# Differences of w_down quarters for the Strassen down projection: made on GpSimd in up passes 1 and 2 and kept in DRAM, instead of made during the down projection

## The chip, the cores and the metric

One Trainium2 chip, and of it one core. The metric is the device time of one execution in microseconds (us), as the median of several executions. A time in a row of the trace is counted from the start of the profiled span.

## The reference, cut to what matters

The whole is one inference step of a small trunk (one layer, 128 prompt tokens and 2048 latent tokens, width 1024): modulation, an input projection, attention and a state-space scan, an output projection, and then a feed-forward network with a centred convolution of width 3. The change touches the last product of that network only:

```python
def conv_ffn(h, w_up, conv_w, conv_b, w_down):
    ...
    g, val = jnp.split(acc + conv_b, 2, axis=-1)
    return (jax.nn.silu(g) * val) @ w_down

xs = xs + gt2[:, None, :] * conv_ffn(h, w_up[l], conv_w[l], conv_b[l], w_down[l])
y_sample = rms_norm(xs, g_final)
```

w_down has D_FF = 2816 rows and 1024 columns; everything is fp32.

## The kernel before, in words

**How fp32 is multiplied.** An operand is split into two fp32r parts: ScalarE (ACT) copies it into an fp32r tile, VectorE (DVE) subtracts that copy from the original and keeps the rest. Each product then is three matmuls (high x high, high x low, low x high). "A split" below means this pair of one ACT and one DVE instruction on 128 x 512 numbers.

**Up** (`ffn_up`, L1237). h @ w_up is a Strassen-Winograd product with 7 products in the place of 8. It goes over 66 units (c, fb): three passes c over the tokens, in each 22 blocks fb of the 2816 columns. A unit is 7 products (numbers 0 to 6; product 0 of the next unit is issued ahead, between this unit's 4 and 5). In pass 0 the sums of the weights are made and split, and the split tiles are written to DRAM (`wsd`, L1233); passes 1 and 2 only split three blocks per unit (one of them with its subtraction on GpSimd, POOL, L1231) and load the other four tiles from `wsd` (`w<-wsd`, L1228, 512 KB each). The gated result `th` is made on POOL (L1262) twice per unit and stored to `ffd` in DRAM (L1263). In passes 0 and 1, in the blocks 4, 8, 12 and 16, `combos` (L1142) loads 732 KB of tokens of the next pass, makes four differences of 128 x 366 numbers on POOL, and stores 732 KB.

**Down** (`ffn_down`, L1535). ff @ w_down is a Strassen-Winograd product, too. The 22 row blocks of w_down are taken as 11 pairs (block k of the upper half, block k of the lower half); a pair and the two column halves of 512 give four quarters of 128 x 512: two of the upper half (columns left and right) and two of the lower half. Three passes p take 3, 4 and 4 pairs (`KS`, `K0`, L64). Within a pass the 16 latent token blocks are taken two at a time as units u = 0 to 7, and u = 8 is the prompt. A step (p, u, g) is product g (0 to 6) of a unit: 9 matmuls per step in pass 0 and 12 in passes 1 and 2 (`down_product`, L1522). Units 0 and 1 (with 8 in pass 0) are interleaved step by step, and so are 6 and 7 in passes 0 and 1; the order is `down_steps`, L1389.

Product g needs its weights `dW[g, k]` (split tiles) for each pair k. Products 0, 1 and 5 use a quarter as it is; 2, 3, 4 and 6 use differences of quarters. These are made in the down stage: `down_fetch` (L1427) loads quarters into three raw places, `down_split` (L1433, instructions on L1438 ACT and L1439 DVE) splits one, and `down_sum` (L1441, instruction on L1444) subtracts in place, on POOL, or on DVE for two of the four in passes 1 and 2. `down_builds` (L1446) writes the order out: splits, sums and a few late fetches, each waiting for the one before it in the same raw place. They are issued two or three per step by `some` (L1634, called on L1685), for pass p + 1 as soon as the last unit pair of pass p has used a weight tile (`through`). For pass 0 the quarters are fetched at the end of up (L1308, L1313, L1314).

The token side: `down_prep` (L1493) makes the operand of a step as a split (`da`, `stg`: L1483 ACT, L1484 DVE) and changes the raw tokens between operands with two POOL instructions at g = 0 (L1503, L1504) and two at g = 3 (L1506, L1507); `down_tasks` (L1487) gives each its lead in steps. The results go from the PSUM banks X, Y, Z through ACT (`snap`, L1588) and DVE (`put`, L1621 to L1627) into tiles x; in passes 0 and 1 POOL starts an accumulating DMA of x into `x1d` (L1624), and x is free when that has landed. There are three such tiles in pass 0 (L1547).

**What sets the order.** PE, ACT, DVE and POOL run their instructions in the order of the program (L1940); each queue waits at its head. The SP queue, which starts nearly all DMAs, is ordered by the compiler's own schedule, and it waits at its head as well.

Of the kernel before, what the change touches and what calls it, by code (L numbers as in the profile page):

```python
# [9 lines left out]
F32 = mybir.dt.float32  # L10
# [7 lines left out]
D = 1024  # L18
# [57 lines left out]
class Kernel:  # L76
# [1160 lines left out]
    def ffn_up(self, first, p, pp, xp):  # L1237
# [46 lines left out]

        for u, (c, fb) in enumerate(units):
# [6 lines left out]
            if fb in (4, 8, 12, 16) and c < 2:  # L1292
                if fb == 4:
                    todo = self.combos(c + 1)
                next(todo)
            z = pp.tile([128, 512], F32, name="Z", bufs=3)
# [101 lines left out]
    def down_room(self):  # L1398
# [9 lines left out]
        self.dR = [None, None, self.upr.tile([128, 4, 512], F32, name="S", bufs=1)]  # L1408
# [4 lines left out]
        self.dW = {(n // 3, n % 3): pair[:, 1024 * n:1024 * n + 1024].rearrange("p (a c) -> p a c", a=2) for n in range(5)}  # L1413

    def down_raws(self):

        for n in (0, 1):
            t = [self.upr.tile([128, 8, 128], F32, name="upraw", bufs=4).rearrange("p a b -> p (a b)") for _ in range(2)]
            self.dR[n] = t

    def down_quarter(self, p, n, k):
        if n == 3:
            n, k = (0, (k + 3) % 4) if p else ((0, 3), (1, 3), (0, 0))[k]
        t = self.dR[n]
        return t[:, k] if n == 2 else t[k // 2][:, 512 * (k % 2):512 * (k % 2) + 512]

    def down_fetch(self, p, n, row, col, ks=None):  # L1427

        for k in range(KS[p]) if ks is None else ks:
            r0 = (11 * row + K0[p] + k) * 128  # L1430
# [572 lines left out]
```

## Time and profile before

| what | us |
|---|---|
| median of 3 runs | 2597.81 |
| lowest and highest of the 3 | 2597.65, 2606.19 |
| the profiled execution's own time | 2601.17 |
| its span, first to last instruction | 2599.4 |
| up passes 1 and 2 in the span, about | 1475 to 2109 |
| down in the span, about | 2109 to 2599 |

The rows further down come from the profiled execution. A row of a timeline has the start in us, the time taken, the engine, the source line, the operation, the tiles (written <- read), shape and number; in brackets stands how long the engine was idle before it and which instruction released it. A row of stretches has, for each engine, busy us and in brackets the number of instructions.

### The profile page before, as it was taken

How to read it: one execution, taken by the hardware profiler on the slowest of the kernel's cores; microseconds unless marked ns; L12 is line 12 of the kernel's file. 1: busy time of each engine (PE TensorE's matmuls, PEld its weight loads, DVE VectorE, ACT ScalarE, POOL GpSimd, SP SyncE). 2: the span in 40 equal slices, each digit the busy share in tenths (PEclk: the TensorE clock that was granted, in tenths of full speed). 3: DMA queues.
4: the chain of work that ended last, by engine and by line, in shares of the span. 5: the costliest groups of instructions: out<-in, count | busy, mean ns of one | idle time of the engine just before them, and what ended most of it. 6: DMA issues, size and time to landing. Idle time of an engine off the chain costs nothing.

```text
span 2599.4 us, 38577 instructions
## 1 busy us (share of the span) xinstructions
PE 2370.9 (91%) x12997; PEld 2091.8 (80%) x12997; DVE 1949.3 (75%) x3283; ACT 1409.3 (54%) x2894; POOL 1290.9 (50%) x1565
## 2 busy tenths in 40 slices
PE   6976997799999878879999999999999999899998
PEld 3765786588888557669999899998999978688787
DVE  6899766887777796778888866666666676966986
ACT  6643556877777575665555644445444453433443
POOL 2687403667767754756666533234222255635343
PEclk8988998899999999989999999999999999999999
DMA  7554754411111547977777877778667658575653
GB/s 243 175 165 147 208 158 132 161 60 68 68 66 46 118 135 257 262 215 253 266 257 252 301 258 264 243 278 293 225 228 245 220 167 178 114 189 100 176 186 110
DMA packets 281368, 486.63 MB, mean 187 GB/s; under 512 B 43737, under 2 KB 166737, under 8 KB 281041
## 3 DMA queue, kind: packets, MB, share of 16 engines
q1 hardware_dynamic: 266481, 457.41, 54.1%
q0 software_dynamic: 9792, 17.83, 4.6%
q10 hardware_dynamic: 4896, 8.92, 1.0%
q8 instruction: 103, 1.69, 0.3%
q14 instruction: 96, 0.79, 0.1%
HBM read 318.84 MB, written 162.86 MB: 185 GB/s over the span
## 4 chain that ended last, share of the span: by engine, by line
PE 47%; DVE 15%; ACT 7%; issue 7%; DMA 4%; POOL 4%; SPq 0%; ACTq 0%; POOLq 0%; DVEq 0%
PE X L1197 13%; PE X L1528 7%; PE Z L1197 6%; PE Z L1528 4%; PE Y L1197 4%; PE pt L1009 3%; DVE w L1231 2%; PE ps L858 2%; PE pt L886 2%; ACT w L1230 1%; DVE dw L1439 1%; PE Y L1528 1%; PE pm L280 1%; PE po L890 1%; PE po L891 1%
## 5 line engine op out<-in xcount | busy, mean ns | idle before, releaser
L1197 PE MATMUL X<-T,w 128*128 128x366 f32 x3168 | 561.4, 333 | 20.9 <-ACT s L1267 20.7
L1197 PEld LDWEIGHTS X<-T,w 128*128 128x128 f32 x3168 | 538.1, 191 | 26.1 <-ACT s L1267 25.1
L1197 PE MATMUL Z<-T,w 128*128 128x366 f32 x1584 | 289.2, 331 | 6.8 <-DVE Y L1343 3.4
L1197 PEld LDWEIGHTS Z<-T,w 128*128 128x128 f32 x1584 | 267.7, 189 | 11.7 <-DVE Y L1343 6.7
L1262 POOL TENSOR_TENSOR th<-th,v 128x363 f32<-128x363 f32 x132 | 129.6, 982 | 284.2 <-DVE th L1258 204.9
L1231 POOL TENSOR_TENSOR w<-upraw,w 128x512 fp32r<-128x512 f32 x66 | 89.4, 1354 | 235.5 <-DVE v L1251 132.5
L194 DVE SCALAR_TENSOR_TENSOR wacc<-wa,scf,wacc 128x256 f32<-128x256 f32 x224 | 164.3, 778 | 13.0 <-ACT wacc L196 7.8
L1267 ACT ACTIVATE s<-X 128x366 f32<-128x366 f32 x198 | 93.9, 474 | 128.9 <-PE X L1197 128.9
L1528 PE MATMUL X<-dw,da 128*128 128x512 f32 x573 | 144.6, 398 | 9.3 <-DVE da L1484 4.9
L897 DVE TENSOR_TENSOR pTl<-pt,pTh 128x512 fp32r<-128x512 f32 x158 | 108.1, 684 | 50.3 <-ACT pTh L896 48.7
L1197 PE MATMUL Y<-T,w 128*128 128x366 f32 x792 | 144.9, 332 | 0.0
L239 POOL TENSOR_SCALAR ssq<-ssq 128x1 f32<-128x1 f32 x68 | 23.3, 343 | 239.7 <-ACT xn L238 94.5
L624 POOL TENSOR_TENSOR fm<-HS,A 128x544 f32<-128x544 f32 x64 | 92.0, 1438 | 95.9 <-DVE HS L606 80.2
L1528 PEld LDWEIGHTS X<-dw,da 128*128 128x128 f32 x573 | 108.8, 191 | 36.3 <-DVE da L1484 6.6
L1197 PEld LDWEIGHTS Y<-T,w 128*128 128x128 f32 x792 | 135.9, 191 | 0.0
L860 DVE CUSTOM_DVE_ANT_0 sm<-ps,mask,nsink 128x640 f32<-128x640 f32 (+2 forms) x136 | 112.7, 830 | 28.8 <-PE ps L858 28.6
L1484 DVE TENSOR_TENSOR da<-T,da 128x512 fp32r<-128x512 f32 (+1 forms) x111 | 87.7, 796 | 48.3 <-ACT da L1483 48.0
L1230 ACT ACTIVATE w<-upraw 128x512 fp32r<-128x512 f32 x198 | 123.2, 622 | 0.0
L847 ACT ACTIVATE sm<-sm,nm 128x640 f32<-128x640 f32 (+2 forms) x136 | 107.6, 791 | 27.5 <-DVE nm L860 27.2
L1798 PE MATMUL aq<-win,hT 128*128 128x512 f32 x408 | 114.7, 419 | 0.0
L1798 PE MATMUL au<-win,hT 128*128 128x512 f32 x408 | 108.3, 407 | 6.8 <-DVE hT L1729 5.3
L1231 DVE TENSOR_TENSOR w<-upraw,w 128x512 fp32r<-128x512 f32 x132 | 112.9, 855 | 0.3
(586 smaller groups left out, 6175.6 us busy)
## 6 DMA issues: line engine op xcount, KB each, us to landing
w<-wsd SPq DMA_DIRECT2D x176, 512.0 KB, 7.7
upraw<-in_w_up_dram SPq DMA_DIRECT2D x88, 512.0 KB, 6.2
wsd<-w SPq DMA_DIRECT2D x88, 512.0 KB, 5.6
ffd<-th SPq DMA_DIRECT2D x132, 181.5 KB, 2.5
wa<-in_w_ada_dram SPq DMA_DIRECT2D x64, 256.0 KB, 3.1
T<-ffd SPq DMA_DIRECT2D x32, 512.0 KB, 7.8
upraw<-in_w_up_dram SPq DMA_DIRECT2D x44, 256.0 KB, 4.2
upraw<-in_w_down_dram SPq DMA_DIRECT2D x44, 256.0 KB, 5.5
```

The source lines that it names most:

```text
L194: V.scalar_tensor_tensor(o, raw[:, k % RK], g, o, op0=OP.mult, op1=OP.add)
L624: e.tensor_tensor(m, ev[:, :, ::-1] if n else ev, A[n], op=OP.mult)
L847: S.activation(out[hh][:, :W], out[hh][:, :W], AF.Exp, scale=-1.0, bias=nm[:, hh:hh + 1], accum_out=l[:, hh:hh + 1])
L860: V.tensor_tensor_reduce(t[:, :W], ps[:, c0:c0 + W], mask, -1.0, self.nsink[:, h:h + 1], op0=OP.add, op1=OP.min, accum_out=nm[:, hh:hh + 1])
L897: V.tensor_tensor(lo, pv, hi, op=OP.subtract)
L1197: self.T.matmul(bank[:, :NI], w[:, a, k], t[:, b, k, :NI], start=(first and k + n == 0), stop=(k == 3 and n == 2), skip_group_check=True)
L1230: S.activation(w[:, 0], x, AF.Copy)
L1231: (G if n in WP7 else V).tensor_tensor(w[:, 1], x, w[:, 0], op=OP.subtract)
L1262: G.tensor_tensor(th, th, v, op=OP.mult)
L1267: S.activation(s[:, :NI], x[:, :NI], AF.Copy)
L1528: self.T.matmul(bank, a[:, x, k], self.dW[g, k][:, y], start=(first and k + m == 0), stop=(k == n - 1 and m == 2), skip_group_check=True)
L1798: T.matmul(t, hT[:, a, k, :], w[:, k, b, c0:c0 + t.shape[1]], start=(k + a + b == 0), stop=(k == 7 and a == 1))
```

## The change

- Eleven units of the up passes 1 and 2 (`sums`) load one pair of w_down's row blocks (`quarters_load`: two DMAs of 512 KB) into the tile S. In the unit after, POOL makes the four differences in place, two after product 4 and two after product 5 (`quarters_sums`), and SP stores the 1 MB to a new DRAM tensor `wdd`.
- Down has no sums. Each of the 21, 28 and 28 weights of a pass is loaded (256 KB) from w_down or from `wdd` into one of eight places in four `upraw` tiles and split from there; the load of the weight after the next seven is issued behind each split (`down_begin`, `down_fetch`, `down_some`).
- Splits go out 2 per step in the first 18 steps of pass 0, then 1 and 2 in turn; three already in the last up unit and five at the start of down.
- The two subtractions at g = 3 in `down_prep` move from POOL to DVE for units 6, 7 of passes 0 and 1 and units 0, 1 of passes 1 and 2.
- The tile S, no longer needed for raw quarters in down, gives three more tiles x (six in pass 0). Some weight and operand tiles change places; the number of operand places stays.

The diff, cut:

```diff
@@ ffn_up
+        sums = [(1, fb) for fb in range(2, 19, 4)] + [(2, fb) for fb in range(1, 17, 3)]
         for u, (c, fb) in enumerate(units):
...
+            if (c, fb) in sums:
+                self.quarters_load(sums.index((c, fb)))
+            summed = sums.index((c, fb - 1)) if (c, fb - 1) in sums else None
...
                 if c == 2:
                     self.down_room()
-                    self.down_fetch(0, 2, 0, 0)
                     for i in (8, 0, 1):
                         self.down_load(0, i)
             if down == 0:
-                self.down_raws()
-                self.down_fetch(0, 0, 1, 0)
-                self.down_fetch(0, 1, 0, 1)
+                self.down_begin(0)
             product(u, 1, y, True)
...
-            if down == 1:
-                self.down_split(0, 0, 2, [0, 1])
             product(u, 4, x)
             s3 = snap(x, "s3")
+            if summed is not None:
+                self.quarters_sums(summed, 0, 2)
             V.tensor_tensor(y[:, :NI], z[:, :NI], s3[:, :NI], op=OP.add)
+            if down == 1:
+                self.down_some(3)
             step()
...
             if down == 1:
-                self.down_split(0, 0, 2, [2])
-                self.down_split(0, 1, 0, [0])
-                self.down_fetch(0, 3, 1, 1)
-                for k in range(KS[0]):
-                    self.down_sum(0, k, 2, 1, 2)
+                self.down_run(-1)
             step()
             product(u, 5, x)
             step()
...
+            if summed is not None:
+                self.quarters_sums(summed, 2, 4)
             v1 = taps(x, 1, fb, "v1")
             gated(t1, v1, 2 * c, fb)
@@ new functions (in the place of down_raws, down_quarter, down_fetch, down_split, down_sum, down_builds)
+    def quarters_load(self, kk):
+        self.quarters = self.upr.tile([128, 4, 512], F32, name="S", bufs=1)
+        for h in range(2):
+            r0 = (kk + 11 * h) * 128
+            self.Q.dma_start(self.quarters[:, 2 * h:2 * h + 2].rearrange("p a c -> p (a c)"), self.I["w_down"][0, r0:r0 + 128])
+    def quarters_sums(self, kk, n0, n1):
+        q = self.quarters
+        for o, x, y in ((0, 1, 0), (1, 3, 1), (3, 3, 0), (2, 2, 3))[n0:n1]:
+            self.G.tensor_tensor(q[:, o], q[:, x], q[:, y], op=OP.subtract)
+        if n1 == 4:
+            self.Q.dma_start(self.wdd[kk], q)
+    def down_begin(self, p):
+        if p == 0:
+            self.draws = [self.upr.tile([128, 8, 128], F32, name="upraw", bufs=4).rearrange("p a b -> p (a b)") for _ in range(4)]
+        self.dnext = [(p, g, k) for g in range(7) for k in range(KS[p])]
+        self.dloaded = []
+        self.dthrough = set(range(7) if p == 0 else ())
+        for n in range(8):
+            self.down_fetch(self.draws[n // 2][:, 512 * (n % 2):512 * (n % 2) + 512])
+    def down_fetch(self, q):
...
+        src = self.I["w_down"][0, r0:r0 + 128, 512 * (g == 5):512 * (g == 5) + 512] if n is None else self.wdd[kk][:, n]
+        self.Q.dma_start(q, src)
+        self.dloaded.append((p, g, k, q))
+    def down_some(self, n):
+        while n and self.dloaded and self.dloaded[0][1] in self.dthrough:
+            p, g, k, q = self.dloaded.pop(0)
+            w = self.dW[g, k]
             self.S.activation(w[:, 0], q, AF.Copy)
             self.V.tensor_tensor(w[:, 1], q, w[:, 0], op=OP.subtract)
+            self.dbuilt.add((p, g, k))
+            self.down_fetch(q)
+            n -= 1
@@ down_prep
-        tt = self.G.tensor_tensor
+        tt = (self.V if g == 3 and u in (0, 1, 6, 7) and (p, u // 2) not in ((0, 0), (2, 3)) else self.G).tensor_tensor
@@ ffn_down
-        free = [self.mo0, self.dextra, wp.tile([128, 512], F32, name="dx")]
+        free = [self.dS[:, n] for n in range(3)] + [self.mo0, self.dextra, wp.tile([128, 512], F32, name="dx")]
...
-        builds = self.down_builds(0)[7:]
         self.down_run(0)
-        for _ in range(8):
-            builds.pop(0)[1]()
-        self.down_run(-1)
+        self.down_some(5)
...
             if s == (p, 2, 0) and p < 2:
-                self.down_fetch(p + 1, 2, 0, 0)
-                self.down_fetch(p + 1, 0, 1, 0)
-                self.down_fetch(p + 1, 1, 0, 1)
+                assert not self.dnext and not self.dloaded
+                self.down_begin(p + 1)
...
             if p < 2 and u == 7:
-                if g == 0:
-                    builds, through = self.down_builds(p + 1), set()
-                through.add(g)
+                self.dthrough.add(g)
...
             if n > 1:
-                some(3 if p and u < 2 else 2)
+                self.down_some(2 if p == 0 and n < 18 else 1 + n % 2)
```

## Rows read from the trace of the kernel before

**Rows 1.** The page: the span.

```profile
span 2599.4 us, 38577 instructions
```

**Rows 2.** Stretches: length; busy (count) PE, PEld, DVE, ACT, POOL; clock; DMA share; GB/s.

```profile
1514.00:1528.00 14.00, 14.00 (x85) 14.00 (x85) 8.56 (x16) 6.33 (x12) 3.25 (x3) 1.00 0.66 232
1542.00:1556.00 14.00, 14.00 (x86) 14.00 (x85) 9.02 (x16) 6.41 (x12) 5.86 (x6) 1.00 0.78 275
...
2109.00:2132.00 23.00, 18.38 (x71) 13.14 (x70) 21.46 (x27) 11.05 (x22) 15.75 (x12) 0.91 0.23 74
2132.00:2160.00 28.00, 27.57 (x117) 22.38 (x115) 22.99 (x33) 11.69 (x25) 16.30 (x16) 0.96 0.95 243
...
2205.00:2240.00 35.00, 35.00 (x153) 28.29 (x153) 27.80 (x37) 17.14 (x34) 19.57 (x19) 1.00 0.57 121
2240.00:2272.00 32.00, 23.11 (x87) 17.25 (x86) 31.86 (x34) 13.45 (x25) 22.96 (x19) 0.89 0.58 125
2272.00:2370.00 98.00, 98.00 (x434) 81.16 (x433) 60.20 (x86) 29.23 (x52) 39.96 (x38) 1.00 0.72 166
...
2405.00:2442.00 37.00, 32.88 (x135) 25.78 (x133) 36.76 (x42) 13.43 (x26) 22.63 (x18) 0.95 0.61 142
```

**Rows 3.** Timeline of PE: use of a loaded tile in up, then two waits.

```profile
2084.65 2.17 PE L1197 MATMUL X<-T,w 128*128 128x366 f32 x12
...
2252.15 4.18 PE L1528 MATMUL X<-T,da 128*128 128x512 f32 x9 [5.85 <-DVE dx L1623]
...
2438.01 4.15 PE L1528 MATMUL X<-dw,da 128*128 128x512 f32 x10 [1.45 <-DVE da L1484]
```

**Rows 4.** Timeline of DVE in down: one plain subtraction and two long ones.

```profile
2242.89 0.68 DVE L1484 TENSOR_TENSOR da<-T,da 128x512 fp32r<-128x512 f32 x1
...
2251.93 5.04 DVE L1484 TENSOR_TENSOR da<-T,da 128x512 fp32r<-128x512 f32 x1
...
2420.38 5.11 DVE L1484 TENSOR_TENSOR stg<-T,stg 128x512 fp32r<-128x512 f32 x1
```

**Rows 5.** Timeline of POOL beside the first long one, and ACT behind it.

```profile
2251.41 1.57 POOL L1444 TENSOR_TENSOR upraw<-upraw 128x512 f32<-128x512 f32 x1
...
2253.24 3.12 POOL L1444 TENSOR_TENSOR upraw<-upraw 128x512 f32<-128x512 f32 x2
...
2259.76 1.68 POOL L1506 TENSOR_TENSOR T<-T 128x512 f32<-128x512 f32 x1 [1.24 <-DVE stg L1484]
...
2261.47 0.63 ACT L1483 ACTIVATE stg<-T 128x512 fp32r<-128x512 f32 x1 [10.52 <-POOL T L1506]
```

**Rows 6.** Groups by line from 1900 us on: busy, mean ns, idle before.

```profile
L1444 POOL TENSOR_TENSOR S<-upraw,S 128x512 f32<-128x512 f32 x14 | 21.2, 1647 | 5.6 <-DVE T L1439 2.8 <-DVE dw L1439 2.8
L1444 POOL TENSOR_TENSOR upraw<-upraw 128x512 f32<-128x512 f32 x11 | 18.3, 1815 | 0.0
```

**Rows 7.** Stretches of L1439 alone: length, DVE busy us (instructions), clock, DMA.

```profile
2205.00:2240.00 35.00, 13.80 (x11) 1.00 0.57 121
2240.00:2272.00 32.00, 12.12 (x11) 0.89 0.58 125
```

**Rows 8.** Timeline of POOL in one plain up unit of pass 1.

```profile
1747.04 1.29 POOL L1231 TENSOR_TENSOR w<-upraw,w 128x512 fp32r<-128x512 f32 x1 [4.56 <-ACT w L1230]
1750.02 0.97 POOL L1262 TENSOR_TENSOR th<-th,v 128x363 f32<-128x363 f32 x1 [1.69 <-issue]
```

**Rows 9.** Timeline of the SP queue: up units, then the start of down.

```profile
1568.41 5.84 SPq L1263 DMA_DIRECT2D ffd<-th  x2
...
2075.78 1.36 SPq L1228 DMA_DIRECT2D w<-wsd  x3
...
2117.24 19.92 SPq L1431 DMA_DIRECT2D upraw<-in_w_down_dram  x5
```

**Rows 10.** DMA issues by tiles: number, KB each, median us to landing.

```profile
w<-wsd SPq DMA_DIRECT2D x176, 512.0 KB, 7.7
...
upraw<-in_w_down_dram SPq DMA_DIRECT2D x44, 256.0 KB, 5.5
```

More of the change, by code (lines that the diff above doesn't have):

```diff
@@ L1407, in down_room @@
         self.dfree = [flat(self.stg.tile([128, 4, NR], F32R, name="stg", bufs=2))[:, :1024] for n in range(2)]
-        self.dR = [None, None, self.upr.tile([128, 4, 512], F32, name="S", bufs=1)]
+        self.dS = self.upr.tile([128, 4, 512], F32, name="S", bufs=1)
         self.dbuilt = set()
@@ L1412, in down_room @@
         self.dgate, self.dextra = [pair[:, 5120:5632].bitcast(F32), units[0]], units[1]
[L1413 to L1425, printed above, removed]
@@ L1427, in down_fetch @@
-    def down_fetch(self, p, n, row, col, ks=None):
-        for k in range(KS[p]) if ks is None else ks:
-            r0 = (11 * row + K0[p] + k) * 128
-            self.Q.dma_start(self.down_quarter(p, n, k), self.I["w_down"][0, r0:r0 + 128, 512 * col:512 * col + 512])
-    def down_split(self, p, g, n, ks=None):
-        for k in range(KS[p]) if ks is None else ks:
-            w, q = self.dW[g, k], self.down_quarter(p, n, k)
-            self.dbuilt.add((p, g, k))
+        self.dW = {(0, n): pair[:, 1024 * n:1024 * n + 1024].rearrange("p (a c) -> p a c", a=2) for n in range(4)}
@@ new lines, in down_room @@
+        self.dspare = [pair[:, 3072:4096]]
+        self.dfree.append(pair[:, 4096:5120])
+    def quarters_load(self, kk):
[9 more added lines that the diff above has]
+            self.Q.dma_start(self.wdd[kk], q)
@@ new lines, in down_begin @@
+    def down_begin(self, p):
[7 more added lines that the diff above has]
+    def down_fetch(self, q):
+        if not self.dnext:
+            return
+        p, g, k = self.dnext.pop(0)
+        kk = K0[p] + k
+        n = {2: 3, 3: 0, 4: 1, 6: 2}.get(g)
+        r0 = (kk + 11 * (g > 0)) * 128
+        src = self.I["w_down"][0, r0:r0 + 128, 512 * (g == 5):512 * (g == 5) + 512] if n is None else self.wdd[kk][:, n]
+        self.Q.dma_start(q, src)
+        self.dloaded.append((p, g, k, q))
@@ L1438, in down_split @@
+    def down_some(self, n):
+        while n and self.dloaded and self.dloaded[0][1] in self.dthrough:
+            p, g, k, q = self.dloaded.pop(0)
+            w = self.dW[g, k]
             self.S.activation(w[:, 0], q, AF.Copy)
             self.V.tensor_tensor(w[:, 1], q, w[:, 0], op=OP.subtract)
-    def down_sum(self, p, k, *places):
-        o, x, y = [self.down_quarter(p, n, k) for n in places]
-        e = self.V if p and places[0] + places[1] in (2, 5) else self.G
-        e.tensor_tensor(o, x, y, op=OP.subtract)
@@ L1446, in down_builds @@
-    def down_builds(self, p):
-        def split(g, n):
-            return [(g, lambda k=k: self.down_split(p, g, n, [k])) for k in range(KS[p])]
-        def sums(g, *places):
-            return [(g, lambda k=k: self.down_sum(p, k, *places)) for k in range(KS[p])]
-        def fetch(g, *which):
-            return [(g, lambda: self.down_fetch(p, *which))]
-        out = split(0, 2) + sums(0, 2, 1, 2) + split(1, 0)
-        if p:
-            out += fetch(1, 3, 1, 1)
-        late = [split(2, 2), sums(3, 1, 3, 1)]
-        return (out + split(3, 2) + sums(3, 2, 3, 2) + late[p > 0] + late[p == 0] + split(4, 1) + fetch(4, 1, 1, 0)
-                + split(5, 3) + sums(5, 1, 1, 2) + split(6, 1))
+            self.dbuilt.add((p, g, k))
@@ L1632, in put @@
             later.append(square(i, bank, ssq, parts, len(parts)))
-        def some(n):
-            while n and builds and builds[0][0] in through:
-                builds.pop(0)[1]()
-                n -= 1
-        banks, through = {}, set(range(7))
+        banks = {}
         fill()
@@ L1880, in run @@
             self.td = dp.tile([3, 4, 128, 4, NI], F32, name="td")
+            self.wdd = dp.tile([11, 128, 4, 512], F32, name="wdd")
             self.wsd = dp.tile([22, 4, 128, 2, 4, 128], F32, name="wsd")
```

35 lines of the change are left out of this document (16 added, 19 removed).

## The prediction

> **What bounds the kernel now.** I read the stretches first, then the timelines where a stretch showed PE short, then the groups by line. In the up passes the reader is to see PE busy 14.00 of 14.00 us, unit after unit, also in the unit that `combos` loads most [rows 2]: nothing can be gained there, only lost. In down, 2272 to 2370 shows PE at its full rate, 98.0 us for 434 matmuls, 0.226 us each [rows 2]. Held against that rate three places are short: 2109 to 2160 has 188 matmuls, 42.5 us of work in 51, so 8.5 us lost (the start, T0); 2205 to 2272 has 240, 54.2 in 67, so 12.8 lost (pass 0 to 1, T1); 2405 to 2442 has 135, 30.5 in 37, so 6.5 lost (pass 1 to 2, T2) [rows 2]. Together 27.8 us: the most that the change can give. In T1 and T2 the loss includes the clock, granted at 0.89 and 0.95 [rows 2], which falls where PE has waited: the nine matmuls behind the 5.85 us wait took 4.18 us [rows 3].
>
> In T1 and T2 DVE is busy 31.86 of 32 and 36.76 of 37 us [rows 2]: it is the engine that PE waits for, as the wait of 5.85 us for a `put` and the later one for an operand show [rows 3]. Part of that busy time isn't work. A subtraction of 128x512 takes 0.68 us, yet at 2251.93 one takes 5.04 and at 2420.38 one takes 5.11 [rows 4]; beside the first POOL runs sums back to back [rows 5]. On L1439 the 22 splits of T1 took 25.9 us [rows 7], where 22 x 0.68 is 15.0: 10.9 us too long, with 4.4 at 2251.93 about 15 us of the 59.7 that DVE was busy there. The sums also delay POOL's own token work: ACT waits 10.52 us for L1506, which came only when the sums were through [rows 5].
>
> After the row, the rule: the Trainium skill (GPSIMD Engine Reference, section 1, Specifications) says that GpSimd shares its SBUF interfaces with VectorE and contends with its instructions that have two SBUF inputs. Both subtractions above have two, so the trace agrees. The rule also speaks against this change, since sums in the up passes meet VectorE there; that is rival 4.
>
> **The change part by part.**
>
> *Sums out of down.* 28 sums go from POOL (25 of them in the rows: 39.5 us, 1.65 to 1.82 each [rows 6]) and 16 from DVE. In exchange DVE gets 8 units x 2 = 16 subtractions of `down_prep` in the transitions, at 0.68 [rows 4]. DVE's count is thus unchanged, and nothing is gained from its own work; what it loses is the contention. In T1 POOL is busy 19.57 + 22.96 = 42.5 us [rows 2]. Eight sums at 1.57 [rows 5] are 12.6 of them, and eight moved token subtractions, four of 384 columns, at an estimated 1.4 (below the 1.68 of L1506 [rows 5]) are 11. So 23.6 of 42.5, 55%, goes. T2 loses as much. In T0 the 12 sums of pass 0 are some 20 us at 1.65 [rows 6], of which about 15 fall into POOL's 32 us there [rows 2]; units 0 and 1 of pass 0 keep their subtractions on POOL. About half goes.
>
> If PE's loss fell only in step with POOL's work, T1 would keep 45%, 5.8 us; if DVE's backlog fitted inside the lead of four to six steps that operands have, about 1. DVE's work without the 15 us is 45 us in 67, so a backlog of a few us remains only in the dense half; I take 4. T2, by the same ends of 2.9 and 0.5, 2. T0, ends of 4.3 and 1, 3.5, as POOL still makes its first token subtractions. What is left is 9.5 of 27.8: **18 us gained**, 15 by the upper ends and 25 by the lower.
>
> *Splits.* 77 before and after, on the same two engines: nothing. Spread to 1.5 per step they are through 28/1.5 = 19 steps after product 0 of unit 7, before product 3 of the next pass's first pair; product 6 needs the last of them four to six steps later. So the rate is no new wait as long as the loads come.
>
> *Loads.* 77 loads of 256 KB in the place of 44. Eight stand ready at each transition; the ninth is issued behind the first split and needed eight splits later, 5.3 steps of 2.0 to 2.7 us, 11 to 14 us, against 5.5 us to land [rows 10]. In T0 two splits per step take 512 KB in 2.0 us, 250 GB/s, about what the queue moved in 2132 to 2160 (243 [rows 2]); there a load may be late by 2 to 3 us, which is in the 3.5 above. SP is held by loads even now, 19.92 us at 2117.24 [rows 9], so a waiting load ahead of token loads is not new. Cost: 0, up to rival 3.
>
> *Three more tiles x.* DVE waits less for accumulating DMAs in pass 0; these waits cost PE nothing outside T0. Nothing.
>
> *Sums into up.* 11 units get four POOL subtractions, 6.6 us at 1.65, where POOL is busy 3.25 of 14 [rows 2]. Two go into the gap of 4.56 us ahead of L1231. The other two stand ahead of `gated`, where the gap is 1.69 us [rows 8], so `th` comes 1.6 us later. Behind it on SP stands its store, then the second store, for which SP waits anyhow: 5.84 us for the pair [rows 9]. That covers 1.6. For DVE, the `combos` unit shows POOL 2.61 us busier and DVE 0.46 [rows 2]; at that ratio 6.6 us of sums cost DVE 1.2 us per unit, of 5.4 idle. If the cover were gone, these 1.2 x 11 = 13 us would be on the path.
>
> *Loads and stores into up.* 11 loads and 11 stores of 1 MB, in different units. A tile from `wsd` is issued at 2075.78 [rows 9] and used at 2084.65 [rows 3]: 8.9 us, against 7.7 to land [rows 10], a slack of 1.2. At the 232 GB/s of a plain unit [rows 2] 1 MB takes 4.5 us. The `combos` unit moves 732 KB in and 732 KB out (275 GB/s) without a PE gap, more than one load or one store of 1 MB; so I take **0.5 us in all**, between 0 and rival 2. The last load of pass 1, at block 18, coincides with token loads of the next pass: that is the 0.5.
>
> *The sum.* 18 - 0.5 = 17.5 us. The profiled execution took 2601.17 us (span 2599.4 [rows 1]), 3.4 above the median of 2597.81; the differences hold for either. 2597.8 - 17.5 gives **2580 us**.
>
> **The rivals.**
>
> 1. *DVE stays full.* The order of splits, puts and operands is dense without the contention, too: in pass 0's half of T1, 20 splits, some 14 operands and 14 instructions of the results are 48 of up to 0.68 us, at most 33 us, in 13 steps of 9 x 0.226 = 26.5. Against it: the half behind has room. If half or less of the expected gain came, 8 us: 2590.
>
> 2. *Up waits for `wsd`* (the slower side). A queue of DMAs with 1 MB ahead delays the tile of product 2; one place, `w<-wsd` in the unit with the load. Price: 4.5 - 1.2 = 3.3 us x 11 = 36, and with the stores' units up to twice that. It decides from 1.6 us per unit, where it eats the 17.5. With loads alone: 2580 + 36 = 2616. Against it stands the `combos` unit; for it, the slack of 1.2.
>
> 3. *The ring runs dry.* Each load waits on SP for a split, and behind it stand the token loads; each T keeps half of its loss by waits for loads in the place of waits for POOL, another 5 us on top of the 9.5, and T0 all of its 8.5: 2580 + 10 = 2590, and to 2600 where the transitions get as bad as now. For it: 243 GB/s in T0 at a DMA share of 0.95 [rows 2].
>
> 4. *Sums hold DVE in up as in down.* By the rows at 2251.93 one subtraction was held for the whole run of sums; held for all 6.6 us, DVE in a unit would lack 6.6 - 5.4 = 1.2 us of room, 13 us in 11 units: 2593. This is what the rule of the GPSIMD Engine Reference in the Trainium skill would make of it, at its strictest. The `combos` unit, 0.46 for 2.61, speaks against it.
>
> That the change doesn't do what it says has no room: the sums' operands and stores are explicit.
>
> **How the numbers follow.** A measurement of this kernel tells about 0.5%, 13 us, from no change. Forecast 0.55; rival 1, 0.20; rival 2, 0.10; rival 3, 0.10; rival 4, 0.05. Faster by over 13 us: nearly all of the forecast, whose own range is 2571 to 2585 (gains of 25 to 15, widened by 2 us for up), and a quarter of rival 1: 0.60. Within 13 us: the rest of rivals 1, 3 and 4, and the mild half of rival 2's delays: 0.28. Slower: the rest of rival 2 and a little of 3: 0.12. The range for 8 in 10 goes from 2568 (all of the 27.8, and 2 us for the scatter of runs) to 2600 (rivals 1, 3, 4), leaving out rival 2.
>
> **What would show it.** Right: in the stretches around both transitions 0.226 us per matmul nearly throughout, no L1484 or split subtraction above 2 us, no wait of ACT for L1506 above 4 us; 44 POOL subtractions of S in passes 1 and 2, with PE 14.00 of 14.00 in their units; DVE there about 1 us busier. Wrong: idle time of PE behind `w<-wsd` or ACT in up (rivals 2, 4); ACT's splits waiting for DMA in T0, T1, T2 (rival 3); DVE full in the transitions with every instruction at 0.68 us (rival 1).

## The result, and the profile after

The kernel after takes 2574.55 us (median of 4 runs, 2572.71 to 2574.73), the kernel before, on the same chip, 2599.61 (2597.65 to 2606.19). The ratio is 0.9898, with a 95% interval of 0.9878 to 0.9917. The profiled execution took 2574.71 us.

The page of the kernel after, span and engines; the span answers to [rows 1]:

```profile
span 2572.9 us, 38713 instructions
...
PE 2360.7 (92%) x12997; PEld 2088.9 (81%) x12997; DVE 1908.3 (74%) x3283; ACT 1409.7 (55%) x2894; POOL 1290.4 (50%) x1565
```

Stretches of the kernel after, with the columns of [rows 2]. The first four are units of up pass 1 (the one with the first load of quarters, the one with the first two of its four sums, the next one with the other two beside differences of `combos`, and one in which a load meets the traffic of `combos`), the others the three places in down. This execution reached down 5 us earlier than that of before, so the stretches lie as much later in the work.

```profile
1505.00:1519.00 14.00, 14.00 (x85) 14.00 (x84) 8.60 (x15) 6.41 (x12) 3.20 (x4) 1.00 0.65 226
1519.00:1533.00 14.00, 14.00 (x86) 14.00 (x85) 8.61 (x15) 6.41 (x12) 6.27 (x6) 1.00 0.66 230
1533.00:1547.00 14.00, 14.00 (x86) 14.00 (x85) 8.91 (x15) 6.41 (x12) 9.81 (x10) 1.00 0.79 299
1547.00:1561.00 14.00, 14.00 (x86) 14.00 (x85) 8.61 (x15) 6.41 (x12) 3.19 (x4) 1.00 1.05 396
...
2104.00:2155.00 51.00, 48.69 (x212) 39.15 (x211) 42.01 (x67) 25.40 (x51) 22.66 (x23) 1.00 0.79 205
2205.00:2240.00 35.00, 30.55 (x131) 24.98 (x130) 29.63 (x49) 20.71 (x41) 12.01 (x12) 0.95 0.89 234
2240.00:2272.00 32.00, 32.00 (x135) 26.25 (x135) 23.27 (x38) 13.44 (x24) 4.98 (x6) 0.95 0.93 228
2405.00:2442.00 37.00, 37.00 (x165) 30.63 (x164) 32.87 (x52) 17.64 (x39) 3.37 (x10) 1.00 0.68 211
```

By the prediction's yardstick of 0.226 us per matmul, T0 now lacks 51 - 212 x 0.226 = 3.1 us (8.5 before), T1 67 - 266 x 0.226 = 6.9 (12.8), T2 nothing (6.5). In the stretch where DVE had been busy 31.86 of 32 us [rows 2] it is busy 23.27, and POOL 4.98 in the place of 22.96.

The line of the sums in the kernel after: all 44 are on POOL, in up.

```profile
L1429 POOL TENSOR_TENSOR S<-S x44: 1289/1298/1822, 1527.7 to 2049.5; 128x512 f32<-128x512 f32 x44
```

Timelines of the kernel after: PE in block 18 of pass 1, the only unit of passes 1 and 2 away from their boundaries that got longer, then PE, ACT, DVE and the SP queue in T1.

```profile
1734.25 2.25 PE L1197 MATMUL X<-T,w 128*128 128x366 f32 x12 [0.37 <-DMA w<-wsd]
...
2237.84 5.46 PE L1530 MATMUL X<-T,da 128*128 128x512 f32 x12 [4.45 <-DVE S L1623]
...
2225.03 0.63 ACT L1485 ACTIVATE da<-T 128x512 fp32r<-128x512 f32 x1 [2.95 <-DMA T<-ffd]
2231.53 0.63 ACT L1485 ACTIVATE da<-T 128x512 fp32r<-128x512 f32 x1 [5.34 <-DMA T<-ffd]
...
2232.19 0.69 DVE L1486 TENSOR_TENSOR da<-T,da 128x512 fp32r<-128x512 f32 x1 [3.80 <-ACT da L1485]
...
2208.10 10.52 SPq L1452 DMA_DIRECT2D upraw<-wdd  x9
2219.27 0.92 SPq L1478 DMA_DIRECT2D T<-ffd  x2
...
2221.72 1.58 SPq L1478 DMA_DIRECT2D T<-ffd  x2
```

Timelines of the kernel before, DVE and POOL ahead of the `put` for which PE waited 5.85 us [rows 3]:

```profile
2230.15 4.07 DVE L1439 TENSOR_TENSOR T<-upraw,T 128x512 fp32r<-128x512 f32 x2
...
2230.21 2.85 POOL L1444 TENSOR_TENSOR S<-upraw,S 128x512 f32<-128x512 f32 x2
```

What is left in T1 has another cause than before. Before, DVE worked from 2230.15 until that `put` without a break, on instructions that were in part held, as the two splits shown. After, ACT waits at its head for tokens, 2.95 and 5.34 us; their loads were issued only at 2219.27 and 2221.72, behind nine weight loads. DVE stands idle for ACT, and the same `put` comes 4.45 us late.

**One table for all kernels.** Each row is one profiled execution; the times of the runs stand with the experiments. "Up to end" runs from the first matmul of up to the end of the span. Ahead of that the kernels do the same work, yet the 14 executions reach it anywhere between 1120 and 1132 us, so this column compares more closely than spans do. A loss is worked out from the starts of down's 1980 matmuls in the trace: each step over 0.26 us, less 0.2267, summed (T0: matmuls 0 to 200, T1: 420 to 700, T2: from 1120 on). It counts a little more than the prediction's stretches, 31.6 us in the place of 27.8, since it sees also what lies between them. "DVE over 0.7" sums what DVE's instructions in T1 took above 0.7 us each; "POOL busy in T1" sums what POOL's took, its starts of DMAs among them. Executions scatter: after, e2, e4, e5 and e6a make the same operands and splits in T1 and lose between 5.4 and 7.2 us there, so a difference of under 2 us in T1 tells nothing by itself. In T0 the same five differ by 0.1.

| kernel | up to end | T0 | T1 | T2 | DVE over 0.7 | POOL busy in T1 |
|---|---|---|---|---|---|---|
| before | 1473.0 | 10.0 | 13.0 | 8.6 | 19.0 | 44.1 |
| after | 1450.3 | 3.4 | 7.2 | 0 | 1.1 | 19.4 |
| b2_sums_aside | 1475.2 | 10.7 | 14.0 | 8.2 | 15.1 | 42.5 |
| e1_g3_pool | 1449.6 | 3.3 | 6.3 | 0 | 5.1 | 30.1 |
| e3_dummy_sums | 1467.0 | 14.7 | 10.4 | 0.8 | 7.4 | 33.3 |
| e9_one_input | 1460.5 | 11.6 | 7.8 | 0 | 3.2 | 34.6 |
| e11_both_back | 1473.2 | 14.3 | 12.1 | 4.1 | 11.5 | 43.4 |
| e2_x_three | 1450.6 | 3.4 | 6.3 | 0 | | 19.4 |
| e4_no_up_sums | 1450.2 | 3.5 | 5.4 | 0 | | |
| e6a_up_pool | 1455.1 | 3.4 | 5.8 | 0 | | 19.4 |
| e5_up_double | 1470.0 | 3.4 | 5.7 | 0 | | 19.4 |
| e7_pace | 1447.8 | 3.4 | 3.0 | 0 | 1.1 | 19.7 |
| e8_lead | 1447.4 | 3.4 | 2.0 | 0 | 2.7 | 20.0 |
| e10_lead_pace | 1446.1 | 3.3 | 1.3 | 0 | 2.6 | 17.6 |

From before to after "up to end" falls by 22.7 us: 21.4 in down, 0.9 in up passes 1 and 2 (630.6 to 629.7) and 0.4 in pass 0. The other 3.8 us between the two spans lie ahead of up and are scatter. So is what up seems to gain: the nine kernels with the up passes of the kernel after take 628.4 to 631.0 us for passes 1 and 2.

T1 has two parts, up to the `put` named above and behind it. The kernel before lost 6.8 and 6.1 us in them, the kernel after 4.6 and 2.6, b2 6.9 and 7.1, e3 7.8 and 2.6, e11 9.4 and 2.7. T2 of the kernel before includes 1.8 us somewhat farther on in pass 2; the expectations count it without them, as 6.8.

### The profile page after: what moved, and what is told of

The parts are those of the page before. It is cut to its first block, busy times and chain, and to the rows that moved or that the text cites. A ratio compares the mean times of both kernels' runs of the same rounds, so it can differ in the third digit from the quotient of the medians.

```text
span 2572.9 us, 38713 instructions
## 1 busy us (share of the span) xinstructions
PE 2360.7 (92%) x12997; PEld 2088.9 (81%) x12997; DVE 1908.3 (74%) x3283; ACT 1409.7 (55%) x2894; POOL 1290.4 (50%) x1565
## 4 chain that ended last, share of the span: by engine, by line
PE 51%; DVE 12%; ACT 7%; issue 5%; DMA 5%; POOL 4%; SPq 0%; ACTq 0%; POOLq 0%; DVEq 0%
PE X L1197 13%; PE X L1530 9%; PE Z L1197 6%; PE Z L1530 5%; PE Y L1197 3%; PE pt L1009 3%; DVE w L1231 2%; PE ps L858 2%; PE Y L1530 2%; PE pt L886 2%; ACT w L1230 1%; DVE ha L689 1%; PE po L890 1%; PE po L891 1%; DVE pTl L897 1%
## 5 line engine op out<-in xcount | busy, mean ns | idle before, releaser
L1197 PEld LDWEIGHTS X<-T,w 128*128 128x128 f32 x3168 | 537.8, 191 | 27.8 <-ACT s L1267 26.2
L194 DVE SCALAR_TENSOR_TENSOR wacc<-wa,scf,wacc 128x256 f32<-128x256 f32 x224 | 164.3, 778 | 11.6 <-ACT wacc L196 7.1
L886 PE MATMUL pt<-ident,sm 128*128 128x128 f32 x632 | 100.3, 278 | 12.6 <-ACT sm L847 7.8
L896 ACT ACTIVATE pTh<-pt 128x512 fp32r<-128x512 f32 x158 | 93.5, 592 | 29.2 <-PE pt L886 28.6
L1249 ACT ACTIVATE g<-Z,vec 128x363 f32<-128x363 f32 x66 | 43.3, 655 | 118.2 <-DVE Z L1375 118.2
```

What stands on the lines that cost most here:

```text
L194: V.scalar_tensor_tensor(o, raw[:, k % RK], g, o, op0=OP.mult, op1=OP.add)
L886: T.transpose(pt[:, hh], sm[hh][:, j * 128:(j + 1) * 128], self.ident)
L1197: self.T.matmul(bank[:, :NI], w[:, a, k], t[:, b, k, :NI], start=(first and k + n == 0), stop=(k == 3 and n == 2), skip_group_check=True)
```

## The experiments

### Is it the sums' work or their order? (b2, on the kernel before)

The sums write a tile that nobody reads, so that no split waits for a sum; 44 two-input subtractions stay, 384 columns wide and every third made twice.

```diff
-        e.tensor_tensor(o, x, y, op=OP.subtract)
+        o = self.aside[0 if e is self.G else 1]
+        self.asides[e is self.G] += 1
+        for _ in range(2 if self.asides[e is self.G] % 3 == 0 else 1):
+            e.tensor_tensor(o, x[:, :384], y[:, :384], op=OP.subtract)
```

> The kernel before, but every sum of down writes its result aside (128x384, every third made twice, so the same columns) and the splits read the raw quarters: POOL and DVE do the same amount of work, and nothing waits for a sum any more (the differences of w_down are left out of the result). Before: 480.8 us from the first to the last matmul of down, lost at the start T0 10.0, at T1 13.0, at T2 6.8. Theory as first stated (the sums' work holds DVE and POOL): 476 to 481, losses nearly as before. Theory after the run with idle POOL work (T0 is lost to POOL's work, T1 and T2 to the chain in which ACT and DVE stand behind sums): T0 stays near 10, T1 falls to 5 to 8, T2 to 0 to 2; down 466 to 472. Rival (all is the chain): T0 below 5, down 462 or less.

Measured: 2601.75 us (2596.76 to 2609.57), a ratio of 1.0003 to the kernel before, interval 0.9991 to 1.0015. Down takes 482.2 us, 1.2 above the bound of the first theory, with the losses much as before; the second theory (T1 5 to 8) and the rival are out. Waits of the kernel b2 in T1, for PE and for ACT:

```profile
PE X L1533 <- DVE dx L1628: 6.2, 1, 6.2
```
```profile
ACT stg L1488 <- POOL T L1511: 8.7, 1, 8.7
```

Without any wait for a sum the same two waits stand there as in the kernel before (5.85 and 10.52 us [rows 3, 5]). So it isn't the chain of sums and splits that costs: it is their work. The run keeps the sums of both engines and the old order of loads, so it doesn't tell POOL's sums from DVE's.

### POOL's work put back, part by part (e3, e9, e1, e11, on the kernel after)

e3 puts idle two-input subtractions back where sums used to stand; POOL's 32 instructions there write a tile that nobody reads.

```diff
             self.down_fetch(q)
             n -= 1
+            if self.scr is not None and k == KS[p] - 1 and g in ((0, 1, 2, 3) if p == 0 else (0, 3)):
+                for _ in range(KS[p] + 1):
+                    self.G.tensor_tensor(self.scr, self.dgate[0][:, :384], self.dgate[1][:, :384], op=OP.subtract)
```

> The changed kernel with POOL work put back into down that nobody waits for: 12 subtractions of 128x384 in pass 0 and 10 behind splits of each later pass (in runs of 4 or 5, at the places where the sums stood; numbers from the gate tiles, result to a scratch tile). Theory (POOL's instructions hold DVE and POOL's own token work): down 8 to 15 us longer than 459.4, with single splits on DVE of 3 us and more in both transitions. Rival (the gain came from the chain load, sum, split, late load, which is gone here too): under 3 us longer.

Measured: 2593.11 us (2591.97 to 2594.16), 0.9959 of before (0.9944 to 0.9974). Down takes 474.9 us where the kernel after takes 459.4: idle work, of which nobody needs a result, brings back 15.5 of 21.4 us, a little over the 8 to 15 expected. The splits of 3 us and more that were expected with it didn't come: the longest DVE instruction in T1 took 1.92 us, in T2 1.95. And it doesn't bring the losses back where they were: T0 loses 4.7 us more than before, T2 7.8 less. The line of the idle work, and the waits of ACT and of PE in T0 (each its sum, its number and the longest):

```profile
L1468 POOL TENSOR_TENSOR scr<-T x32: 992/1343/1466, 2115.0 to 2425.3; 128x384 f32<-128x384 f32 x32
...
ACT stg L1489 <- POOL T L1512: 8.7, 2, 5.9
...
PE X L1534 <- ACT stg L1489: 4.7, 1, 4.7
```

In T0 POOL's token subtraction stands behind the idle work, ACT stands waiting for it, and PE for ACT. The same rows of the kernel after have POOL at 4.2 us in 2 waits and no such wait of PE.

e9 is e3 with one input in the place of two; the line by which they differ:

```diff
-self.G.tensor_tensor(self.scr, self.dgate[0][:, :384], self.dgate[1][:, :384], op=OP.subtract)
+self.G.tensor_scalar(self.scr, self.dgate[0][:, :384], 2.0, None, op0=OP.mult)
```

> The kernel after, with the same 30 idle POOL instructions in down as e3_dummy_sums (12 in the start, 9 at each later transition, in runs of four or three), but of one input, a multiplication by a constant, on the same 384 columns. The product goes to a tile that nobody reads. e3 lost 15 us of down and its DVE instructions were longer than 0.7 us by 7.4 us in T1, against 1.1 in the kernel after. Theory A, DVE is held by POOL instructions with two inputs: one input holds it less, DVE's surplus in T1 is under 2.5 us, T0 loses 3 to 5 and T1 6 to 8, down takes 458 to 462 us and the time is 2573 to 2578. Theory B, the queue: what costs is that POOL's token subtractions stand behind the idle work, whatever its inputs: T0 loses 9 to 15 and down takes 467 to 476, the time is 2583 to 2593; if the instruction is shorter than e3's 1.28 us, less in proportion. Theory C, both: DVE's surplus falls, yet ACT still waits over 4 us for POOL's T in T0, and T0's loss lies between 5 and 10.

Measured: 2587.22 us (2585.22 to 2594.21), 0.9946 of before (0.9929 to 0.9963). The same rows of the kernel e9:

```profile
L1468 POOL TENSOR_SCALAR scr<-T x32: 1169/1430/1720, 2121.8 to 2427.7; 128x384 f32<-128x384 f32 x32
...
ACT stg L1489 <- POOL T L1512: 8.3, 2, 5.5
...
PE X L1534 <- ACT stg L1489: 4.6, 1, 4.6
```

The instruction occupies POOL a little longer than e3's (median 1430 ns to 1343), so the comparison is fair to the queue; there are 32 of them, 10 at each later transition and not 9 as the expectation says. The two costs come apart. **The queue:** T0 still loses 11.6, with the same wait of ACT for POOL; that is 8.2 of the 11.3 us by which e3 worsens T0. **The hold on DVE:** its time over 0.7 us in T1 falls from 7.4 to 3.2, and T1 loses 7.8, near the 7.2 of the kernel after; so some 2.6 us of e3's 10.4 need the second input, not far beyond the scatter. SP shows the way: behind each split stands the load of a later weight, and the nine weight loads ahead of the tokens take 13.20 us in e3 and 10.90 in e9, where the kernel after has 10.52. The same rows of the kernels e3 and e9:

```profile
2223.53 13.20 SPq L1453 DMA_DIRECT2D upraw<-wdd  x9
...
2227.07 10.90 SPq L1453 DMA_DIRECT2D upraw<-wdd  x9
```

This fits a held DVE that delays splits, the loads behind them and so the tokens; no run separates it from the hold on the results themselves. None of the three theories holds to the letter. C names the two parts rightly, but its bound for T0, 5 to 10, is too low.

e1 puts the moved token subtractions of g = 3 back on POOL, and e11 has both e1 and e3.

```diff
-        tt = (self.V if g == 3 and u in (0, 1, 6, 7) and (p, u // 2) not in ((0, 0), (2, 3)) else self.G).tensor_tensor
+        tt = self.G.tensor_tensor
```

> The changed kernel, but the 16 token subtractions of product 3 in the transitions go back from DVE to POOL. In the changed kernel the down stage takes 459.4 us from its first matmul to its last (before: 480.8). Theory (what counts is that POOL runs less beside DVE, and that what DVE must wait for comes sooner): 16 x 1.4 = 22 us of POOL work return into T0, T1 and T2, about as much as half of what the sums were, DVE gets 11 us back; down 3 to 8 us longer, mostly in T1 and T2. Rival (the moved subtractions were the gain, the sums mattered little): 12 us or more longer. Rival (they do not matter): under 1 us.

> The kernel after with both parts of POOL's old work back in down: the idle subtractions of e3_dummy_sums (12 in the start, 10 at each later transition) and the token subtractions of g = 3 on POOL as in e1_g3_pool. POOL is then about as busy in T1 as in the kernel before (44.1 us; e3 33.3, e1 30.1, after 19.4), while the weights still come from DRAM and nothing waits for a sum. Theory that the amount of POOL work behind and beside the tokens is what cost the transitions: T1 loses 10 to 14 and T2 3 to 7, DVE's surplus over 0.7 us in T1 is 12 or more (before 19.0, e3 7.4), down takes 476 to 484 and the time is 2594 to 2604, within 0.3% of the kernel before. Rival, that the two parts matter only one at a time, and T2's loss came from the order of sums and splits in the kernel before: T2 loses under 2, T1 10 to 11, down 472 to 476, time 2590 to 2595, as e3. A third way, that DVE freed of 16 subtractions gives back what POOL costs: T1 under 10, time under 2590.

Measured: e1 2578.26 us (2573.99 to 2585.32), 0.9905 of before (0.9885 to 0.9925), its transitions as good as those after: the theory of 3 to 8 us is out, the last of its rivals holds. e11 2599.21 us (2596.85 to 2608.18), 0.9993 of before (0.9979 to 1.0007): the time of the kernel before, though its weights come from DRAM and its sums are made in up. Its time, T1 and T2 lie where the first theory had them, DVE's surplus a little under (11.5 for 12). Waits of the kernel e11: PE's and two of ACT's in T1, then ACT's in T2.

```profile
PE X L1534 <- DVE S L1628: 9.2, 1, 9.2
...
ACT da L1489 <- DMA T<-ffd: 10.7, 2, 5.8
ACT stg L1489 <- POOL T L1512: 9.2, 1, 9.2
...
ACT T L1489 <- POOL T L1512: 7.5, 1, 7.5
```

The equal time is in part a coincidence. T0 loses 4.3 us more than before, T1 0.9 and T2 4.5 less, and T1's loss is made otherwise: ahead of the late `put` ACT waits 10.7 us for tokens, as in the kernel after, and its wait of 9.2 us for POOL ends only behind it, where e11 loses 2.7 us and the kernel before 6.1. So e3 and e11 show that POOL's work beside the transitions costs as much as the change gained; they don't show that it cost the kernel before in the same places.

The two parts don't add: alone, e1's 11 us of POOL work per transition cost nothing (DVE is freed of the same subtractions there), beside the idle sums they cost another 4.4 us of down (479.3 to 474.9), 3.3 of them in T2. Operands are made some steps ahead; that POOL's lateness costs only where it exceeds that lead fits this, but no run varies the two against each other. e11's T2 loses 4.1 of the 8.6 us that the kernel before loses; its POOL work is much the same there (37.7 us to 38.2), but its sums are 384 columns wide and DVE makes none. Which of the two accounts for the rest wasn't tried.

### Three more tiles x (e2) and the sums in up (e4)

e2 takes three of the tiles x away again until pass 1. e4 makes no sums in up and loads other columns of w_down in their place, so products 2, 3, 4 and 6 of down have other weights.

```diff
-        free = [self.dS[:, n] for n in range(3)] + [self.mo0, self.dextra, wp.tile([128, 512], F32, name="dx")]
+        free = [self.mo0, self.dextra, wp.tile([128, 512], F32, name="dx")]
...
-        sums = [(1, fb) for fb in range(2, 19, 4)] + [(2, fb) for fb in range(1, 17, 3)]
+        sums = []
```

> The changed kernel with three tiles x in pass 0 and in the first steps of pass 1, as before (the tile S gives its four only after that). Changed kernel: down 459.4, lost T0 3.4, T1 7.2, T2 0; its relatives lost 5.4 to 6.3 in T1. Theory (waits for accumulating DMAs cost nothing once the sums are gone): within 1.5 us of 458 to 459.5. Rival (the six tiles are what freed T1, where DVE's results wait for x): T1 10 or more, down 3 us or more longer.

> The changed kernel without the loads, sums and stores in the up passes; down loads plain quarters of w_down in the place of the differences (that part of the computation is left out). Theory (the work in up is hidden): up passes 1 and 2 take the same time within 1 us, down the same 459.4 within 1 us, the whole within 2 us of the changed kernel. Rival (up pays for them): 4 us or more faster in up. Rival (the loads from the new tensor are slower than loads from w_down): down 2 us or more faster.

Measured: e2 2579.82 us in its one run, e4 2574.58 (2573.65 to 2576.23), 0.989 of before (0.9873 to 0.9906). From up to the end both take what the kernel after takes (1450.6 and 1450.2 to 1450.3 us); e4's down is 1.8 us shorter, outside the 1 us of its theory but within T1's scatter. The tiles are worth nothing that shows, and the sums, loads and stores in up cost nothing that shows.

### How near was up to its edge? (e5, e6a)

e5 makes each load, each subtraction and each store of the quarters twice; e6a only the subtractions. The second subtraction changes the weights of products 2, 3, 4 and 6. The line common to both (e5's loops around loads and stores are left out):

```diff
+            for _ in range(2):
                 self.G.tensor_tensor(q[:, o], q[:, x], q[:, y], op=OP.subtract)
```

> The changed kernel with the work in up doubled: each pair is loaded twice, each difference made twice in place and each store made twice (the differences come out wrong in value, as the second subtraction works on the first one's result). Per unit 8 POOL instructions and 2 MB. Theory (POOL has 10 us of room in a unit, the queues have some): up 0 to 4 us longer, PE short only behind tiles loaded from DRAM. Rival (the room was nearly used up, the slack of 1.2 us ahead of the loaded weight tiles is the edge): up 10 to 40 us longer.

> The kernel after, where each of the 44 subtractions of quarters in the up passes is made twice (the same tile, so the quarters in DRAM are other numbers), and loads and stores stay single. e5_up_double, with loads and stores doubled too, lengthened passes 1 and 2 by 18 to 19 us (328.0 and 320.8). Theory that the DMA queues are up's edge: passes 1 and 2 take 315 to 317.5 and 312 to 315.5 as before, PE 14.00 of 14.00 in the units with eight subtractions, the time 2572 to 2579. Theory that POOL is the edge (13 us of sums per unit, rival 4 at double): each of the 11 units is 1 us or more longer, passes 1 and 2 together 641 or more, the time 2585 or more.

Measured: e5 2596.61 us (2591.28 to 2599.59), 0.9972 of before (0.9959 to 0.9984); e6a 2580.38 in its one run. Passes 1 and 2 take 648.8 us in e5 and 634.3 in e6a, against 629.7. Stretches of the kernel e5 in pass 1: one in which doubled loads meet the traffic of `combos`, a plainer one, and one with POOL at its busiest. The last row is the kernel e6a's, in block 9 of pass 1.

```profile
1559.00:1573.00 14.00, 12.81 (x77) 12.51 (x76) 6.65 (x13) 5.00 (x10) 1.97 (x2) 1.00 1.03 399
1583.00:1597.00 14.00, 14.00 (x85) 14.00 (x85) 8.61 (x15) 6.35 (x13) 6.24 (x5) 1.00 0.70 234
1601.00:1615.00 14.00, 14.00 (x86) 14.00 (x85) 9.82 (x16) 6.41 (x12) 12.90 (x12) 1.00 0.72 256
...
1612.00:1626.00 14.00, 13.11 (x78) 12.81 (x78) 6.33 (x12) 5.90 (x12) 3.25 (x3) 1.00 1.05 362
```

Waits of DVE and of PE in the first of them, kernel e5:

```profile
DVE th L1258 <- DMA ffd<-th: 4.9, 1, 4.9
...
PE Z L1197 <- DVE Y L1344: 1.2, 1, 1.2
```

Inside the units the edge is the DMA queues, not POOL. With POOL at 12.90 of 14 us PE runs through. Where 399 GB/s are moved at a share of 1.03, DVE waits 4.9 us until the store of `th` has landed, and PE waits for DVE; so e5's rival has the size right, 19 us, but not the place, which it saw ahead of the loaded weight tiles. e6a's row shows the same with POOL at 3.25 of 14 us: DVE waits 4.6 us for the store of `th` there. e6a falls between its two theories, 634.3 us for 641 or more on the one side and 2580.38 for at most 2579 on the other. By the starts of its first matmuls a unit takes 14.05 us; e5's blocks 5 and 6, 9 and 10, 13 and 14, 17 and 18 of pass 1 take 11.1 us more together, and its pass 2 units 0.6. In e6a the units of pass 1 come to 1.7 us over, in the kernel after only block 18, by 0.6 (14.66 us): the place of the row at 1734.25 above. In the other eight kernels with its up passes block 18 is over by 0 to 0.6. The rest of e5's and e6a's lengthening lies about the boundary between the passes, where it isn't settled.

### What is left of T1 (e7, e8, e10)

e7 slows the splits in the back half of pass 0 and quickens them in units 0 and 1 of pass 1, e8 lets the first operands of the next pass be made two steps ahead in the place of four, and e10 does both.

```diff
-                self.down_some(2 if p == 0 and n < 18 else 1 + n % 2)
+                self.down_some(2 if p == 0 and n < 18 else 1 if p == 0 else 2 if p == 1 and u < 2 else 1 + n % 2)
...
-... n - (4 if s[1] == 8 else lead[s[2]] + (s[2] == 3 and s[1] in (0, 1, 6, 7)))
+... n - (4 if s[1] == 8 else 2 if s in ((1, 0, 0), (1, 1, 0)) else lead[s[2]] + (s[2] == 3 and s[1] in (0, 1, 6, 7)))
```

> The changed kernel with one split per step during units 6 and 7 of pass 0 and two per step during units 0 and 1 of pass 1 (before: 1 and 2 in turn in both). Theory for what T1 still loses (the token loads of units 0 and 1 of pass 1, issued at 2219 and 2222 us, land only after 5.7 and 9.7 us because a dozen weight loads stand ahead of them; ACT waits 3.0 and 5.3 us for them, and the results of units 6 and 7 stand behind): fewer weight loads are ahead, T1 falls from 5 to 7 to 3 or less, down 455 or less. Rival (DVE is full there): as much, by less work on DVE. Rival (weights come late at one per step): T1 10 or more.

> The changed kernel with the first operands of units 0 and 1 of pass 1 made two steps ahead and not four, so that they stand behind results of units 6 and 7 on ACT and DVE and not ahead of them; the loads are as they were. Theory (what costs is that ACT and DVE, which work in order, wait for late tokens while results stand behind them): T1 falls from 5 to 7 to 2 or less, down 454 or less. Rival (the tokens themselves come too late for PE): T1 as it was or longer.

> The kernel after with the edits of e7_pace and e8_lead together: one split per step in the back half of pass 0 and two per step in units 0 and 1 of pass 1, and a lead of two steps in the place of four for the first operands of units 0 and 1 of pass 1. Theory that what is left of T1 is the time at which token loads land behind weight loads: e7 had 2.96 of loss there and e8 2.01, and both remove the same wait, so together 1 to 2.5 in T1, down 453.5 to 455, the time 2569 to 2573, the same as either alone within the scatter. Rival, that the later operands and the slower splits meet: put or operands come late in pass 1, T1 loses 5 or more and down takes 457 or more.

Measured: e7 2572.2 us (2569.42 to 2578.91), 0.9897 of before (0.9878 to 0.9915); e8 2571.48 (2569.24 to 2576.58), 0.9897 (0.9879 to 0.9914); e10 2573.07 (2569.3 to 2579.21), 0.9897 (0.9879 to 0.9914). Timeline of the kernel e8, PE and ACT at the place where the kernel after lost 4.45 us:

```profile
2234.61 2.60 PE L1530 MATMUL X<-T,da 128*128 128x512 f32 x10 [0.98 <-DVE da L1486]
...
2220.05 3.46 ACT L1460 ACTIVATE dw<-upraw 128x512 fp32r<-128x512 f32 x6
2224.34 0.63 ACT L1485 ACTIVATE da<-T 128x512 fp32r<-128x512 f32 x1 [0.84 <-DVE dx L1623]
2225.99 0.63 ACT L1485 ACTIVATE da<-T 128x512 fp32r<-128x512 f32 x1 [1.01 <-DMA T<-ffd]
...
2231.89 0.63 ACT L1485 ACTIVATE da<-T 128x512 fp32r<-128x512 f32 x1 [4.47 <-DMA T<-ffd]
```

With a shorter lead ACT does six splits in a row before it comes to the first such operand, and then waits 0.84 us for DVE and 1.01 for tokens, where it had waited 2.95 for the tokens. It still waits 4.47 us for the later tokens, but the `put` is no longer late: PE waits 0.98 us there, for an operand. T1 loses 2.0, with both edits 1.3, and from up to the end 2.5 to 4.2 us go. In the runs' times this doesn't show against the kernel after: the ranges overlap and the ratios differ by 0.0001. DVE has the same work in e8, so its own fullness (e7's rival) isn't the cause. So ACT and DVE standing at late tokens are shown as the cause of most of what T1 still lost, but none of the three is shown to be a faster kernel.

## Why the prediction was right, and where its steps were off

- **The time.** 2580 with 2568 to 2600 was forecast as faster; 2574.55 came. Against 17.5 us, 22.7 came from up to the end. By the starts T0 gave 1.6 us more than forecast, T1 3.1 less and T2 4.1 more. Part of that is the yardstick: the stretches saw 27.8 us lost, the starts 31.6, so 27.8 was not the most that could be had. By the stretches T0 gave 0.4 more, T1 2.9 less and T2 2.0 more. That the sum came near is in part luck: T1's miss and T2's surplus offset each other.
- **T0, 3.5 to be left:** 3.4 by the starts, 3.1 by the stretch. Both causes were named, the hold on DVE first, POOL's queue second, and neither was given its own share of the loss. e9 shows that the queue is the larger here, 8.2 of 11.3 us. Rival 3's sign came, too: ACT's splits wait for `upraw<-wdd` there, 3.3 us in three waits; what they cost PE isn't shown.
- **T1, 4 to be left:** 7.2. The step that failed is that a load may be late only in T0, at 2 to 3 us, and that in T1 loads cost 0. Rival 3 came true in this one place: token loads behind weight loads, some 3 to 5 us by e8 and e10 (5.4 to 7.2 in the kernels without their edits, 2.0 and 1.3 with them). That a waiting load ahead of token loads is not new was true; what the step left out is that here the tokens then land too late, and that ACT stands at its head for them, with splits and, on DVE, results behind.
- **The rows that T1 was read from.** The subtraction of 5.04 us [rows 4] and ACT's wait of 10.52 us [rows 5] lie behind PE's wait of 5.85 us, which was over at 2252.15 [rows 3], so they can't have made it. Ahead of it stand shorter holds: DVE's instructions from 2215 to 2252 take 9.4 us over 0.7 each, those behind 9.5. The change took 2.2 us out of the part ahead and 3.5 out of the part behind.
- **T2, 2 to be left:** 0. The yardstick by stretches saw only 6.5 of the 8.6 us there.
- **The cause.** "What it loses is the contention": the long subtractions are gone (no DVE subtraction over 1.8 us in T1 after, 5.04 before [rows 4]), and the wait of 10.52 us [rows 5] is gone. b2 shows that the work of the sums costs and not the wait for them, e3 and e11 that POOL's work costs in the new kernel. How much of T1 and T2 the kernel before lost to POOL's sums, and how much to the 16 that DVE made itself, stays open. Of the signs named, one was missed by little: ACT still waits once in T2 for L1508, which L1506 has become, 4.3 us where 4 was the bound, and PE doesn't. The rule of the Trainium skill (GPSIMD Engine Reference, section 1, Specifications), that GpSimd contends with VectorE instructions that have two SBUF inputs, agrees with the traces. These add that the number of POOL's own inputs counts, too: 7.4 us over 0.7 in T1 with two, 3.2 with one.
- **The moved subtractions.** Their 11 us of POOL per transition were counted as part of what goes. Alone they are worth nothing (e1); beside the sums 4.4 us (e11 to e3). The step took POOL's work as a sum, of which each us counts alike.
- **Up.** 0.5 us was put at block 18 of pass 1; 0.6 came, there, behind `w<-wsd`, though not in every kernel with these up passes. DVE's 1.2 us per unit did not show: 8.61 in the unit with the first two sums and 8.60 in the plain one, and the 0.31 more in the next falls together with `combos`. With the sums doubled it does show (9.82 us in e5), and still PE runs through: rival 4 is out. Rival 2 priced a load of 1 MB at 3.3 us, beyond a slack of 1.2; e5 loses 0.8 to 2.5 us in a unit where twice that meets `combos`, and in the first of these PE waits 1.2 us for DVE and 0.4 for `w<-wsd`.
- **Rival 1,** DVE full of its own work, is out: DVE is busy 29.63 of 35 and 23.27 of 32 us in T1, and e8 loses 2.0 us with the same DVE work.
- **Splits, tiles x:** nothing, as forecast.

## What to carry to other kernels

Where an engine that is not the bound makes operands for one that is, count its whole queue at each transition against the lead of those operands: here 11 us of such work cost nothing alone and 4.4 us beside more of it. Work off the bottleneck that is moved into an earlier stage with room is then a gain. A long instruction on one engine beside another engine's burst is a sign that the two block each other; swap the burst for one of another kind but of the same length to learn how much is the blocking and how much the queue. When work put back brings back the time, look whether it does so at the same places: in e11 it didn't. When a wait goes, look at once at who stands at the head of each queue: here the loads that took the sums' place delayed the tokens in one of three places.

## What the hardware showed that was not expected

- A POOL multiplication with one input took no less time than a subtraction with two on 128x384 (median 1430 and 1343 ns, e9 and e3), but held DVE less.
- A held DVE subtraction was held through several POOL instructions, not one: 5.04 us from 2251.93 on, while three POOL sums of 1.57 us each ran from 2251.41 on [rows 4, 5]. The Trainium skill (SBUF — State Buffer, "SBUF: two separate sides") says that whichever of the two starts first gets the shared ports for its whole instruction; here DVE, the second, got no turn after the first POOL instruction; it ended at 2256.97, 0.6 us after the third sum.
- A stretch of 14 us at 396 GB/s and a DMA share of 1.05 passed without a gap of PE in the kernel after; 399 GB/s at 1.03 cost PE 1.2 us in e5 and 362 GB/s at 1.05 cost it 0.9 in e6a, where DVE waited for a store. The rate alone doesn't tell.
